# Another order of the steps in both mixers of a two-layer hybrid diffusion backbone

## The chip, the cores and the metric

The kernel runs on one core of one Trainium2 chip. The metric is the device time of one execution in microseconds (us), as the median of several runs. The weights lie in HBM and come in by DMA. Five engines work side by side, each through its own instructions in the order in which they stand in its queue: TensorE (PE, with its weight loads shown apart as PEld), VectorE (DVE), ScalarE (ACT), GpSimd (POOL) and SyncE (SP). They wait for each other by semaphores. An instruction that waits holds back everything behind it on its engine, whether that could run or not.

## What is computed

Two layers work on 256 latent tokens and 256 context tokens of width 1024. Each layer is a half-step feed-forward net (FFN), a mixer, and another half-step FFN; the last mixer and the last FFN work on the latent tokens alone. Cut to the mixer, which is all that the change touches:

```python
def mixer(hx, hc, p, cos, sin, with_ctx):
    qx, kx, vx, ux, gx, bgx, cgx, sx = jnp.split(hx @ p['w_in'], cuts, axis=-1)
    qc, kc, vc, uc, gc, bgc, cgc, sc = jnp.split(hc @ p['w_in'], cuts, axis=-1)
    # group A: attention, 8 query heads, 2 key heads, width 64; q and k RMS-normalised
    qx = apply_rope(head_rms(qx, p['q_g']), cos, sin)
    kx = apply_rope(head_rms(kx, p['k_g']), cos, sin)
    kc = head_rms(kc, p['k_g'])
    attn_x = blocked_attention(qx, concat([kc, kx]), concat([vc, vx]))
    # group B: a linear recurrence in both directions after a width-4 convolution
    hc_f = lru_dir(uc, p, 0, h0, False);  hx_f = lru_dir(ux, p, 0, hc_f[:, -1], False)
    hc_b = lru_dir(uc, p, 1, h0, True);   hx_b = lru_dir(ux, p, 1, hc_b[:, 0], True)
    lru_x = (hx_f + hx_b) * gelu(gx)
    # group C: a gated width-3 convolution
    sc_x = bgx * dw_conv(cgx * sx, p['sc_conv_w'], p['sc_conv_b'], SC_PAD)
    # each group RMS-normalised, concatenated, one projection
    out_x = merge_groups([attn_x, lru_x, sc_x], p['grp_g'], p['w_out'])
    # layer 0 does the same for the context tokens (with_ctx)
```

The two sides of the tokens are called s = 0 (context, 256 keys) and s = 1 (latent, 512 keys) below.

## The kernel before

Activations lie transposed in SBUF, features on the 128 partitions, with context and latent tokens side by side as 512 columns. Every product of fp32 matrices is made of three matmuls in a reduced format (`mm3`, lines 333 to 335): each operand is split into a high part, made by ACT (line 132), and a low part, made by DVE (line 133). This holds for the weights too: a weight block of 128x1024 (512 KB) is fetched by SP into one of seven raw buffers (`dma_to`, four blocks ahead), then ACT makes `hi` and DVE makes `lo`. `get` asks for a block by its name and splits two blocks ahead (`advance`). All blocks are fetched in the order that `plan` fixes; within a mixer `mix_units` walks the table `ORDER` for it, so the blocks of `kv`, `qp`, `sc` and `op` follow the table's order.

PSUM has eight banks of 128x512 fp32, given out in turn by `bank` to whoever asks. A product, a score, a transposition and a statistic take one each, and keep it until ACT or DVE has read it.

A mixer first makes h, the normalised and modulated input (`head`), with the first four blocks of the projection. Then it walks `ORDER[l]` (line 955). Each entry is a step, named by two letters and an index:

- `cv` convolution of the recurrence's input (ACT, DVE); `ga` its gates (two matmuls of 128x512 in fp32 on PE, line 763, then tanh, tanh, tanh, exp and square on ACT); `lr` a logarithm and an exponential (ACT), `ls` the scan (DVE), `le` its end (DVE)
- `ge` gelu (ACT, DVE)
- `kv`, `qp` the key, value and query products (PE, in four held banks each); `ka`, `qa` their statistics; `kb`, `qb` norm, rotation and split of the rows (DVE, ACT); `kc`, `qc` their transposition (PE lines 659 and 697, copied out by ACT)
- `sc` the gated convolution: i % 3 = 0, 1, 2 are its three projections
- `sm` the scores of one head: matmuls (line 832), the row maximum on DVE (`nb`, line 833), the exponential with its sum on ACT (`P`, line 836). In layer 0 `sm0` to `sm7` are side s = 0 and `sm8` to `sm23` side s = 1; layer 1 has `sm0` to `sm15`, all s = 1
- `tr` four transpositions of P on PE (line 846), copied to `PT` by DVE (line 849) and ACT (line 851) by turns
- `va` P times values (line 864, summed in a held bank); `nr` the inverse sums (reciprocal on DVE, two spreads `re` on ACT line 875, eight transpositions on PE line 882, two copies `rec` on ACT)
- `ra`, `rb` norm and merge of the attention group (squares on ACT line 895, statistic on PE line 900); `ma` the statistic of the recurrence's group (`ma1`) and of the convolution's (`ma0`) (squares `acc` and `sq` on ACT lines 359 and 362, statistic on PE line 381, then Ln and Exp on ACT and three steps on DVE); `mb` their scaling and splitting
- `op` one eighth of the output projection of these two groups (12 matmuls); it needs all four `mb`.

After the table the attention group's part of the projection follows. Ln and Tanh lie in different tables of ACT; `tanh` and `ln` (lines 573 and 578) keep them apart and put a table load where the kind changes.

The table gives the order in which the steps are written. A scheduler then places each engine's instructions; where an instruction is not ready by its reckoning it lets later ones pass. So the queue of an engine follows the table, though not word for word.

Of the kernel before, what the change touches and what calls it, by code (L numbers as in the profile page):

```python
# [26 lines left out]


ORDER = (
# [5 lines left out]
    "op5 op6 op7").split(),  # L35
# [3 lines left out]
    "tr13 tr14 tr15 ls2 ls3 le1 nr1 ma1 mb2 mb3 op0 va2 va3 op1 ra1 rb1 op2 op3 op4 op5 op6 op7").split())  # L39


P_BMOD, P_NG, P_GRP, P_FIN = 0, 144, 192, 208
# [1057 lines left out]
```

## Time and profile before

| | |
|---|---|
| median of three runs | 1728.09 us (1726.1 to 1729.63) |
| the profiled execution's own time | 1726.93 us |
| its span | 1725.1 us |
| PE busy | 1645.0 us, 95% of the span |
| DVE busy | 1128.2 us, 65% |
| ACT busy | 661.1 us, 38% |
| mean granted clock of TensorE | 0.981 of full speed |

The span is what the profiler covers, and 1.8 us more lie around it. A busy PE is not a PE at its peak, since its clock changes: 0.50 in a row means the lower of its two levels (1.2 GHz), 1.00 the upper (2.4 GHz). What matters for a change that only moves work is where PE stands idle and what it waits for there. Mixer 0 lies at 425 to 605 us in the span (after its `head`), mixer 1 at 1380 to 1505 us.

### The profile page before, as it was taken

What the parts mean: (1) busy time and instruction counts of PE and PEld (TensorE: products, weight loads), DVE (VectorE), ACT (ScalarE), POOL (GpSimd) and SP (SyncE); (2) the same over time, 40 slices, a digit from 0 to 9 for tenths busy, and PEclk for the clock granted to TensorE, in tenths of its full rate; (3) what the DMA queues carried; (4) which work ended last, traced back from release to release, by engine and by line L of the source; (5) the groups of instructions that cost most, each with busy time, mean ns of one, the idle gap of its engine ahead of it and who ended that gap; (6) DMA issues with size and microseconds to landing.
All of it is one profiled execution on the core that took longest, in us unless ns stands there. A gap on an engine that the chain in (4) does not pass through costs nothing. (4 is left out here: it accounts for less than half of the span.)

```text
span 1725.1 us, 22220 instructions
## 1 busy us (share of the span) xinstructions
PE 1645.0 (95%) x8790; PEld 1394.4 (81%) x8790; DVE 1128.2 (65%) x1869; ACT 661.1 (38%) x1036; POOL 0.2 (0%) x4
## 2 busy tenths in 40 slices
PE   7999999999986999999999999999999988799997
PEld 2888888889764698888888898888888886689997
DVE  4977756675675676686676765664556768575555
ACT  5332122324855443221223252212222359454442
POOL 0000000000000000000000000000000000000000
PEclk9999999999988999999999999999999999899999
DMA  7455645452320024455455424453444332145551
GB/s 292 166 188 185 205 144 179 168 189 90 111 73 13 29 70 159 167 188 181 147 180 179 154 98 147 159 183 113 144 145 157 112 122 86 39 155 186 183 183 39
DMA packets 67937, 246.26 MB, mean 143 GB/s; under 512 B 7668, under 2 KB 8180, under 8 KB 67576
## 3 DMA queue, kind: packets, MB, share of 16 engines
q1 hardware_dynamic: 66816, 243.82, 40.9%
q8 instruction: 69, 1.13, 0.3%
q10 hardware_dynamic: 1016, 1.01, 0.2%
q14 instruction: 36, 0.29, 0.1%
HBM read 243.76 MB, written 1.05 MB: 142 GB/s over the span
## 5 line engine op out<-in xcount | busy, mean ns | idle before, releaser
L132 ACT ACTIVATE hi<-raw 128x1024 fp32r<-128x1024 f32 x310 | 327.2, 1060 | 790.2 <-PE ps L334 593.0
L334 PE MATMUL ps<-hl,hi 128*128 128x512 f32 (+1 forms) x1664 | 584.1, 352 | 0.9 <-DVE hl L418 0.7
L333 PE MATMUL ps<-hh,hi 128*128 128x512 f32 (+1 forms) x1664 | 576.0, 352 | 9.3 <-ACT hh L417 9.1
L335 PE MATMUL ps<-hh,lo 128*128 128x512 f32 (+1 forms) x1664 | 580.9, 350 | 0.0
L133 DVE TENSOR_TENSOR lo<-raw,hi 128x1024 fp32r<-128x1024 f32 x310 | 378.7, 1224 | 195.8 <-ACT hi L132 194.0
L333 PEld LDWEIGHTS ps<-hh,hi 128*128 128x128 f32 x1664 | 313.2, 191 | 53.5 <-ACT hh L417 12.6
L334 PEld LDWEIGHTS ps<-hl,hi 128*128 128x128 f32 x1664 | 317.9, 191 | 43.5 <-DVE hl L418 3.0
L335 PEld LDWEIGHTS ps<-hh,lo 128*128 128x128 f32 x1664 | 317.9, 191 | 40.3
L258 DVE SCALAR_TENSOR_TENSOR junk<-raw,cb 128x1024 bf16<-128x1024 f32 x272 | 321.3, 1221 | 15.3 <-DMA raw<-in_wpk_dram 15.3
L333 PE MATMUL ps<-gh,hi 128*128 128x512 f32 (+1 forms) x770 | 267.7, 348 | 0.0
L334 PE MATMUL ps<-gl,hi 128*128 128x512 f32 (+1 forms) x770 | 267.2, 347 | 0.0
L335 PE MATMUL ps<-gh,lo 128*128 128x512 f32 (+1 forms) x770 | 267.1, 347 | 0.0
L496 DVE TENSOR_TENSOR gf<-gf,ps 128x512 f32<-128x512 f32 (+1 forms) x88 | 54.6, 621 | 182.2 <-PE ps L335 181.0
L333 PEld LDWEIGHTS ps<-gh,hi 128*128 128x128 f32 x770 | 145.9, 190 | 18.1
L334 PEld LDWEIGHTS ps<-gl,hi 128*128 128x128 f32 x770 | 145.9, 189 | 18.1
L335 PEld LDWEIGHTS ps<-gh,lo 128*128 128x128 f32 x770 | 145.9, 190 | 18.0
L426 DVE SCALAR_TENSOR_TENSOR xT<-ps,modT,xT 128x256 f32<-128x256 f32 x160 | 72.5, 480 | 69.0 <-PE ps L335 68.0
L417 ACT ACTIVATE hh<-ht,modT 128x256 fp32r<-128x256 f32 x88 | 41.9, 504 | 70.7 <-DVE ht L416 70.1
L362 ACT ACTIVATE sq<-xT 128x256 f32<-128x256 f32 (+1 forms) x62 | 29.0, 486 | 74.9 <-DVE xT L426 73.5
L133 DVE TENSOR_TENSOR gl<-gf,gh 128x512 fp32r<-128x512 f32 (+1 forms) x88 | 54.5, 620 | 0.7 <-ACT gh L132 0.7
L418 DVE SCALAR_TENSOR_TENSOR hl<-ht,modT,hh 128x256 fp32r<-128x256 f32 x88 | 40.6, 483 | 20.8 <-ACT hh L417 20.6
L333 PE MATMUL ps<-mh,hi 128*128 128x256 f32 (+1 forms) x160 | 50.3, 314 | 3.4 <-ACT mh L132 3.4
(181 smaller groups left out, 1228.3 us busy)
## 6 DMA issues: line engine op xcount, KB each, us to landing
raw<-in_wpk_dram SPq DMA_DIRECT2D x456, 512.0 KB, 3.3
xT<-in_xin_dram SPq DMA_DIRECT2D x2, 1024.0 KB, 9.7
lw<-in_lruw_dram SPq DMA_DIRECT2D x2, 512.0 KB
cb<-in_cc_dram SPq DMA_DIRECT2D x2, 512.0 KB, 3.6
out_dram<-y SPq DMA_DIRECT2D x2, 256.0 KB, 2.6
out_dram<-y ACTq DMA_DIRECT2D x2, 256.0 KB, 2.6
pps<-in_pp_dram ACTq DMA_DIRECT2D x1, 138.0 KB, 4.0
qkb<-in_qkg_dram ACTq DMA_DIRECT2D x1, 128.0 KB
```

What stands on the lines that cost most here:

```text
L132: act(hi, src, AF.Copy)
L133: tt(lo, src, f(hi), OP.subtract)
L258: stt(junk, raw, 1.0, CB[v], op0=OP.mult, op1=OP.mult, accum_out=mod_col(l, m, t, v))
L333: nc.tensor.matmul(ps, wh, xh, start=first, stop=False)
L334: nc.tensor.matmul(ps, wh, xl, start=False, stop=False)
L335: nc.tensor.matmul(ps, wl, xh, start=False, stop=last)
L362: act(sq[:, a:b], src, AF.Square)
L417: act(hh[:, a:b], t[:, a:b], AF.Identity, bias=mod_col(l, 3 * n, k, v))
L418: MADE.append(stt(hl[:, a:b], t[:, a:b], mod_col(l, 3 * n, k, v), f(hh[:, a:b]), op0=OP.add, op1=OP.subtract).ins)
L426: stt(xT[:, k, a:b], ps[:, a:b], mod_col(l, m, k, v), xT[:, k, a:b], op0=OP.mult, op1=OP.add)
L496: tt(gf[:, a:b], gf[:, a:b], pu[:, a:b], OP.mult)
```

## The change

Only the table `ORDER` changes. Both versions hold the same steps, 125 in layer 0 and 97 in layer 1, each once; the functions behind them, the number of instructions apart from table loads, and the bytes moved are the same. The fetch order of the weight blocks follows through `mix_units`: in layer 0 the second `kv` block now comes after two `qp` blocks, and in layer 1 the blocks of `sc0`, `kv1` and `sc1` come before those of `qp1` to `qp3`. ACT's table loads number 16 before and 18 now; both additional ones are in mixer 1.

```diff
 ORDER = (
-    ("cv0 cv1 kv0 kv1 ga0 ga1 ga3 ga2 qp0 qp1 ka0 kb0 kb1 ge0 ge1 qp2 qp3 qa0 qb0 qb1 lr0 lr1 lr2 lr3 sc0 sc1 "
...
+    ("cv0 cv1 kv0 ga1 ga0 ga2 ge0 ga3 qp0 qp1 kv1 lr0 ls0 ka0 kb1 ge1 kb0 qp2 qp3 qa0 qb0 qb1 kc0 kc3 sc0 sc1 "
...
-    ("cv0 kv0 kv1 ka0 kb0 kb1 qp0 qp1 qp2 qp3 qa1 qb2 qb3 ga0 qc4 qc5 qc6 qc7 sc0 cv1 sc1 ge0 sc2 kc0 kc1 kc2 "
...
+    ("cv0 cv1 kv0 ga0 ge0 qp0 ga3 sc0 kv1 ka0 lr3 kb1 sc1 kb0 qp1 qp2 qp3 qa1 qb2 kc2 kc3 kc1 kc0 qb3 qc4 qc5 "
...
```

The rows below are the queues of the built programs, with equal neighbours merged. First ACT in mixer 0, from the second half of the query rows (`qr`) to the first transposed P (`PT`); before:

```order
L132 ACTIVATE hi<-raw 128x1024
L132 ACTIVATE qr<-qo 128x4x64 x4
L836 ACTIVATE P,sums<-ps,nb 128x256 x2
L718 ACTIVATE cg<-ps 128x512
L836 ACTIVATE P,sums<-ps,nb 128x256 x4
L851 ACTIVATE PT<-ps 128x512
```

and now:

```order
L132 ACTIVATE qr<-qo 128x4x64 x2
L718 ACTIVATE cg<-ps 128x512
L836 ACTIVATE P,sums<-ps,nb 128x256 x4
L700 ACTIVATE qT<-ps 128x512
L836 ACTIVATE P,sums<-ps,nb 128x256 x4
L132 ACTIVATE hi<-raw 128x1024
L132 ACTIVATE qr<-qo 128x4x64 x2
L728 ACTIVATE sc<-pd,pps 128x512
L836 ACTIVATE P,sums<-ps,nb 128x256 x6
L132 ACTIVATE hi<-raw 128x1024
L851 ACTIVATE PT<-ps 128x512
```

Before, all four remaining splits of query rows stood ahead of the first exponential; now two do, and fourteen exponentials, of seven heads, stand ahead of the first `PT`.

Next PE in mixer 0, from the first statistic of a group (`acc`, `sq` times `ones`); before:

```order
L381 MATMUL ps<-acc,ones_114 128x512
L381 MATMUL ps<-sq,ones_114 128x512
L832 MATMUL ps<-kT,qT 128x512 x8
L864 MATMUL ps<-PT,vt 64x512 x4
L882 MATMUL ps<-idf,re 128x128 x8
L846 MATMUL ps<-idf,P 128x128 x16
L832 MATMUL ps<-kT,qT 128x512 x4
L900 MATMUL ps<-sq,ones_112 128x256 x4
L832 MATMUL ps<-kT,qT 128x512 x4
L846 MATMUL ps<-idf,P 128x128 x16
L381 MATMUL ps<-acc,ones_114 128x512
L381 MATMUL ps<-sq,ones_114 128x512
```

and now:

```order
L381 MATMUL ps<-acc,ones_114 128x512
L381 MATMUL ps<-sq,ones_114 128x512
L832 MATMUL ps<-kT,qT 128x512 x4
L846 MATMUL ps<-idf,P 128x128 x4
L832 MATMUL ps<-kT,qT 128x512 x4
L846 MATMUL ps<-idf,P 128x128 x12
L882 MATMUL ps<-idf,re 128x128 x8
L381 MATMUL ps<-acc,ones_114 128x512
L381 MATMUL ps<-sq,ones_114 128x512
L832 MATMUL ps<-kT,qT 128x512 x6
L864 MATMUL ps<-PT,vt 64x512 x4
L832 MATMUL ps<-kT,qT 128x512 x6
```

The second statistic has moved forward, next to the inverse sums; the attention group's own statistic (line 900) has moved out of this stretch, to behind `op3`.

Last PE in mixer 1, from the end of the query products (`lo`, `hi` times h) on; before:

```order
L335 MATMUL ps<-hi,hl 128x512
L763 MATMUL ps<-uc,lw 128x512 x2
L697 MATMUL ps<-idr,qr 128x128 x4
L333 MATMUL ps<-hh,hi 128x256
L334 MATMUL ps<-hl,hi 128x256
L335 MATMUL ps<-hh,lo 128x256
```

and now:

```order
L335 MATMUL ps<-hi,hl 128x512
L659 MATMUL ps<-idr,kr 128x128 x16
L697 MATMUL ps<-idr,qr 128x128 x2
L333 MATMUL ps<-hh,hi 128x256
L334 MATMUL ps<-hl,hi 128x256
L335 MATMUL ps<-hh,lo 128x256
```

The sixteen transpositions of keys stand where one gate step stood. The first transposition of query rows still follows directly, ahead of the next projection (`sc3` now, `sc0` before).

## Rows read from the trace of the kernel before

**Rows 1.** The page, its head and its first part: busy time of PE.

```profile
span 1725.1 us, 22220 instructions
PE 1645.0 (95%) x8790; PEld 1394.4 (81%) x8790; DVE 1128.2 (65%) x1869; ACT 661.1 (38%) x1036; POOL 0.2 (0%) x4
```

**Rows 2.** Windows: stretch, length, busy us by engine, granted clock, DMA share, GB/s.

```profile
425.00:605.00 180.00, 151.93 (x754) 116.57 (x753) 116.39 (x212) 108.29 (x221) 0.00 (x0) 0.93 0.17 59
1380.00:1505.00 125.00, 103.71 (x632) 85.34 (x631) 86.52 (x156) 80.53 (x158) 0.00 (x0) 0.90 0.22 76
```

**Rows 3.** PE's waits, 425 to 605 us: us in total, times, longest.

```profile
PE ps L846 <- ACT P L836: 10.2, 4, 8.4
PE ps L882 <- ACT re L875: 7.8, 2, 6.4
PE ps L381 <- ACT acc L359: 7.5, 2, 5.6
```

**Rows 4.** PE's waits, 1380 to 1505 us.

```profile
PE ps L381 <- ACT acc L359: 6.3, 2, 5.1
PE ps L697 <- DVE qr L133: 5.1, 1, 5.1
PE ps L846 <- ACT P L836: 4.6, 2, 2.4
PE ps L333 <- ACT mh L132: 3.4, 1, 3.4
PE ps L882 <- ACT re L875: 1.8, 1, 1.8
```

**Rows 5.** Windows: 256-wide matmuls back to back; then where the granted clock fell.

```profile
1380.00:1385.00 5.00, 5.00 (x44) 5.00 (x43) 0.00 (x0) 0.12 (x1) 0.00 (x0) 1.00 0.00 0
...
1410.00:1415.00 5.00, 0.00 (x0) 0.00 (x0) 4.93 (x14) 1.15 (x4) 0.00 (x0) 0.91 0.39 147
1415.00:1420.00 5.00, 4.93 (x29) 4.94 (x29) 3.07 (x7) 2.56 (x4) 0.00 (x0) 0.50 0.00 1
1420.00:1425.00 5.00, 5.00 (x40) 5.00 (x40) 2.56 (x3) 4.48 (x8) 0.00 (x0) 0.91 0.02 3
495.00:510.00 15.00, 9.25 (x35) 7.29 (x36) 7.01 (x16) 5.01 (x19) 0.00 (x0) 0.66 0.10 36
535.00:545.00 10.00, 5.45 (x28) 5.08 (x28) 3.21 (x5) 7.36 (x16) 0.00 (x0) 0.66 0.00 0
555.00:565.00 10.00, 6.91 (x14) 3.87 (x16) 4.05 (x9) 4.87 (x11) 0.00 (x0) 0.66 0.00 0
1465.00:1475.00 10.00, 5.31 (x20) 4.62 (x20) 7.13 (x16) 3.52 (x10) 0.00 (x0) 0.69 0.00 1
1475.00:1490.00 15.00, 8.59 (x29) 4.96 (x30) 5.82 (x14) 6.50 (x15) 0.00 (x0) 0.64 0.00 1
```

**Rows 6.** Timelines of PE and ACT, 1407 to 1416 us: start, us, instruction.

```profile
1408.07 1.88 PE L763 MATMUL ps<-uc,lw 128*128 128x512 f32 x4
1415.07 0.81 PE L697 MATMUL ps<-idr,qr 128*128 128x128 f32 x4 [5.12 <-DVE qr L133]
...
1414.02 0.72 ACT L132 ACTIVATE qr<-qo 128x256 fp32r<-128x256 f32 x2 [3.12 <-DVE qo L630]
```

**Rows 7.** Timeline of ACT, 438 to 448 us: gates of mixer 0.

```profile
438.81 1.28 ACT L576 ACT_TABLE_LOAD   x1
...
443.48 1.25 ACT L576 ACTIVATE th<-ps,hb 128x512 f32<-128x512 f32 x2
...
446.85 1.25 ACT L576 ACTIVATE th<-ps,hb 128x512 f32<-128x512 f32 x2
```

**Rows 8.** Groups by line, whole span: row maximum, exponential and its sum.

```profile
L833 DVE TENSOR_REDUCE nb<-ps 128x1 f32<-128x512 f32 (+1 forms) x40 | 26.1, 685 | 15.1 <-PE ps L832 15.0
L836 ACT ACTIVATE P<-ps,nb 128x512 f32<-128x512 f32 (+1 forms) x48 | 29.0, 614 | 8.8 <-DVE nb L833 8.8
L836 ACT ACTIVATION_READ_ACCUMULATOR P<-ps,nb 128x1 f32 x48 | 9.8, 205 | 0.0
```

More of the change, by code (lines that the diff above doesn't have):

```diff
@@ L29 @@
 ORDER = (
[5 rows of a table removed]
-    "op5 op6 op7").split(),
[3 rows of a table removed]
-    "tr13 tr14 tr15 ls2 ls3 le1 nr1 ma1 mb2 mb3 op0 va2 va3 op1 ra1 rb1 op2 op3 op4 op5 op6 op7").split())
[5 rows of a table added]
+    "va4 ra1 rb1").split(),
[3 rows of a table added]
+    "va2 ls0 le0 lr2 ls2 le1 ma1 tr3 va3 mb2 va1 mb3 op0 op1 op2 ra1 rb1 op3 op4 op5 op6 op7").split())
 P_BMOD, P_NG, P_GRP, P_FIN = 0, 144, 192, 208
```

12 rows, old and new, of the table ORDER are left out of this document.

## The prediction

> **What bounds the kernel now.** PE does: it is busy for 1645.0 of 1725.1 us [rows 1]. Since the change only moves steps of the two mixers, I read the windows of these two stretches next. In mixer 0 (425 to 605 us) PE is busy for 151.9 of 180 us, in mixer 1 (1380 to 1505 us) for 103.7 of 125 us [rows 2]: 28.1 and 21.3 us of idle time, which is the better part of the 80 us that PE idles at all. DVE and ACT are far from full there (116 and 108 us, 87 and 81 us [rows 2]), so none of the three is a floor: the time goes where one of them stands in front of something that is not ready. PE's waits name the places. In mixer 0 they are a P that comes late (8.4 us at the longest), the spread sums `re` (6.4) and the squares of a group (5.6) [rows 3]; in mixer 1 the squares (5.1), the first query rows (5.1) and a merge (3.4) [rows 4]. Nearly all end on ACT.
>
> **The clock adds to it.** Around six of these waits the granted clock falls to 0.50, the lower level. In the clearest, PE is idle from 1409.95 to 1415.07 us [rows 6]; the clock gives 0.91, 0.50 and 0.91 in the three windows of 5 us [rows 5], that is 6.8 us at the lower level, from 1414.1 to 1420.9, of which 5.8 us after work has begun again. All six places together have 47.6 us at the lower level (twice the length times what is missing to 1.00, summed over the windows [rows 5]). About 5.5 us in each, 33 us in all, are spent working; at half speed that costs 16.5 us, 7.9 in mixer 0 and 8.5 in mixer 1. So 36.0 us in mixer 0 and 29.8 in mixer 1 are lost to order: 65.8 us, the most that a permutation can give.
>
> **What the change costs in itself.** Matmuls, copies and bytes are the same. The weight blocks come in another order, but each is still asked for four ahead, the DMA engines are busy for 0.17 and 0.22 of these stretches [rows 2], and PE waits for no DMA in them [rows 3, 4]: nothing. ACT gets two more table loads in mixer 1, 1.28 us each [rows 7]; 2.6 us, priced with wait (i) below.
>
> The Trainium skill speaks against this edit: ScalarE: Activation LUTs, section Rules for kernel authors, wants all work of one table set done before a switch, and budgets about 2.7 us for each. The trace has 1.28 [rows 7] and decides; by the page's figure the two loads would be 5.4 us, and the gain below smaller by up to 2.8 us.
>
> **What PE will meet instead.** I followed the three queues of the changed program through both mixers with the spacings of the rows: 0.114 us for a 256-wide matmul (44 in 5 us [rows 5]), twice that for 512, one gate on ACT 3.37 us (446.85 - 443.48 [rows 7]), a row maximum 0.69 and an exponential 0.61 with 0.20 for its sum [rows 8]. Where a producer's sum is later than PE's, the difference is a wait. None of them stands in the old trace; the bounds follow the list.
>
> Mixer 0:
> (a) All four gates now stand ahead of the query products, whose four banks come free only with the tanh of the third and fourth gate. ACT needs a load, three gates, a square and a tanh, 1.3 + 10.1 + 0.5 + 0.6 = 12.5 us; PE has three gate steps (1.88 each [rows 6]), 23 narrow and six wide matmuls, 5.6 + 2.6 + 1.4 = 9.6 us. Queued behind are all of `qp` and the rest of `kv1`. About 3.2 us, new.
> (b) `qc2` behind `sc0` and `sc1`: these 48 matmuls and eight transpositions cover 11.8 us, the query rows need about 12.8. 1.0 us.
> (c) The wait of 8.4 us goes: between the scores and the first `tr` now stand 48 projection matmuls (10.9 us), and the exponentials are no longer behind all query rows on ACT.
> (d) The recurrence's statistic still waits for its squares: 1.4 us (before: 7.5 - 5.6 = 1.9 [rows 3]). `tr8` stands close behind `sm9`, whose maximum and exponential (1.3 us) queue behind two others on ACT: 1.6 us. Inverse sums 0.5, second statistic 1.2, `op0` behind the last merge 1.0, the attention statistics 0.5.
> (e) From `op2` on projections lie between everything. Together 10.4 us. My sums go by spacing; a chain loses more at each hop, by an estimate of mine some 0.1 us, five or six hops a wait: 3 us. **13.4 us stay of 36.0.**
>
> Mixer 1:
> (f) The first query transposition still follows the products directly. From the end of the products (1408.07) to the first rows (1415.07) it takes 7.0 us [rows 6]; the cover was one gate step of 1.88, and is now sixteen transpositions, some 1.4. So this wait stays, at 5.5 us, and the clock falls again: 2.9 us.
> (g) Seven scores and a projection fill all eight banks; `sc2` waits for the copy of `sc4`, which ACT makes behind two exponentials: 1.6 us.
> (h) Behind it PE has filler (`sc2`, `sc5`), and the waits for P (4.6 us [rows 4]) go.
> (i) ACT then has two gates (6.7 us), two loads (2.6) and nine exponentials (some 0.66 each) to do, and PE comes to `tr0` and `tr1` ahead of a free bank and of the P of `sm4`: 4.3 us.
> (j) First statistic 1.5, `tr12` 0.5, inverse sums 0.5, second statistic 0.2, `op0` 0.8 (the merge's 3.4 us before [rows 4], since `va` and `tr3` now lie behind the statistic). Together 17.8 us, and 2 us for hops. **19.8 us stay of 29.8.**
>
> Sum: 22.6 + 10.0 = 32.6 us. From the profiled execution's own 1726.9 us this gives 1694.3; the median of the runs shown is 1.2 us above it, so 1696 us (rounded).
>
> Bounds: the short waits, (a) to (e) and (g) to (j), may be covered altogether (the cover in each is within 3 us of the chain), or twice as long (a chain of 6 hops behind a few more entries of ACT's queue). I take the middle because PE is behind its producers at some of them and ahead at others. Nothing here can be a gain beyond 65.8, and (f) does not go.
>
> **Rivals.** *The waits move.* ACT is the engine on which nearly all waits end [rows 3, 4], and its work is unchanged. If the short waits come out twice as long, 13.4 and 11.4 us more are lost and 7.8 us are gained: 1720. For it: PE is now early at many places, each by one or two us. Against: ACT is busy for only 108 of 180 us in mixer 0.
> *All but two go.* Only (f), (a) and (i) stay, 16 us: 49 us gained, 1679. For it: projections between nearly all steps of mixer 0. Against: eight banks.
> *The order does not matter*: PE waits elsewhere for the same sum, 1728. Against: the 8.4 and 5.6 us had nothing in front of them that now has 10.9 us.
> *Slower: the clock stays low.* Between 1475 and 1490 us PE was busy for 8.6 of 15 us, its waits were 1.8, 1.2 and 3.4 us, and the clock was 0.64 [rows 4, 5]. Short waits in a row can thus do what one long one does. If the 25 us from the first statistic to `op0` in mixer 0 and the 25 us before `op0` in mixer 1 run at the lower level, some 20 us of work in each take 40: 40 us lost against 32.6 gained, 1735. [...] Against: the wait of 2.4 us in mixer 1 [rows 4] stands by itself between full stretches, and no fall of the clock goes with it (rows 5 has all six), and PE is busy for four fifths in my sums.
>
> **Chances.** The sum as worked out, a gain of 20 to 44 us: 0.66. Waits move: 0.15. All but two go: 0.08. No change: 0.05. Slower: 0.06. The likeliest gives 1696 us. The range takes the first case (1684 to 1708), most of the second gain and half of the moved waits: 1680 to 1715. A measurement of this kernel tells about 0.2% (3.5 us) from no change; faster by more 0.89, within 0.05, slower by more 0.06.
>
> **What would show it.** In the new profile PE's wait for P ahead of the first `PT` (8.4 us) is gone; the window of mixer 0 shows some 23 us less from its first key product to its end, and at most one dip of the clock; a new wait of line 333 for a tanh stands some 15 us behind the first key products; in mixer 1 line 697 still waits for `qr` by 5 to 6 us with a dip of the clock behind it, and line 846 waits for P or a bank by some 4 us. I am wrong if mixer 0 has waits of over 4 us, if the clock falls there more than once, or if line 697 in mixer 1 no longer waits.

## The result and the profile after

The changed kernel takes 1687.18 us (median of four runs, 1685.05 to 1687.82) against 1727.89 us for the kernel before: a ratio of 0.9766, with a 95% interval of 0.9753 to 0.9778. That is 40.7 us, or 2.3%, less. Measured a second time, it was 0.9779 (0.9764 to 0.9793). The forecast was 1696 us, with a range of 1680 to 1715.

The head of the page of after answers to [rows 1]:

```profile
span 1685.2 us, 22230 instructions
PE 1636.9 (97%) x8790; PEld 1388.3 (82%) x8790; DVE 1126.6 (67%) x1869; ACT 663.4 (39%) x1038; POOL 0.2 (0%) x4
```

PE, DVE and ACT do the same work in a span that is 39.9 us shorter; what went is PE's idle time and its time at the lower clock. To say where, one needs marks that both traces have. PE's statistic over 256 columns at the end of a stage is one. It stands last ahead of mixer 0 and first behind it, and last ahead of mixer 1 and first behind it. The timeline of PE in the kernel before (start, length, instruction):

```profile
401.58 0.60 PE L381 MATMUL ps<-acc,ones 128*128 128x256 f32 x2
...
620.69 0.60 PE L381 MATMUL ps<-acc,ones 128*128 128x256 f32 x2
...
1361.62 0.59 PE L381 MATMUL ps<-acc,ones 128*128 128x256 f32 x2
...
1517.36 0.70 PE L381 MATMUL ps<-acc,ones 128*128 128x256 f32 x2 [0.53 <-DVE acc L366]
```

and in the changed kernel:

```profile
402.49 0.60 PE L381 MATMUL ps<-acc,ones 128*128 128x256 f32 x2
...
591.48 0.60 PE L381 MATMUL ps<-acc,ones 128*128 128x256 f32 x2
...
1332.41 0.59 PE L381 MATMUL ps<-acc,ones 128*128 128x256 f32 x2
...
1477.33 0.70 PE L381 MATMUL ps<-acc,ones 128*128 128x256 f32 x2 [0.53 <-DVE acc L366]
```

From the first mark to the second it was 219.1 us and is 189.0: **mixer 0 gained 30.1 us**. From the second to the third it is 740.9 us in both. From the third to the fourth it was 155.7 and is 144.9: **mixer 1 gained 10.8 us**. Below, the time from the first mark to the end of the span is called the net time: 1323.5 us before (1725.1 - 401.58), 1282.7 after.

The windows of the two mixers in after, as in [rows 2] (mixer 0 up to its first 256-wide products, mixer 1 up to the place that 1505 us was before), and then the windows in which the granted clock fell, as in [rows 5]:

```profile
425.00:576.00 151.00, 145.96 (x764) 114.09 (x763) 114.24 (x204) 107.11 (x215) 0.00 (x0) 0.99 0.22 74
1350.80:1465.00 114.20, 101.61 (x632) 83.32 (x631) 84.98 (x153) 82.73 (x160) 0.00 (x0) 0.93 0.26 88
520.00:525.00 5.00, 3.25 (x14) 2.85 (x14) 3.17 (x5) 3.78 (x9) 0.00 (x0) 0.66 0.00 0
1390.00:1405.00 15.00, 9.56 (x54) 8.09 (x53) 10.16 (x22) 7.15 (x17) 0.00 (x0) 0.77 0.22 70
1425.00:1440.00 15.00, 9.42 (x31) 5.17 (x30) 11.13 (x20) 12.91 (x27) 0.00 (x0) 0.66 0.05 19
```

PE idles for 5.0 us in mixer 0 (28.1 before) and 12.6 in mixer 1 (21.3 before). At the lower level of the clock it spends 3.4 us in mixer 0 (23.8 before) and some 17 in mixer 1 (23.8 before). So 23.1 of mixer 0's 30.1 us are idle time, and PE's busy time between the two marks shrinks by the other 7.0 (191.0 to 184.0 us), for the same matmuls at a higher clock; in mixer 1 it is 8.7 and 2.1.

PE's waits in after, first in mixer 0, then in mixer 1 (line and what it waited for: us in total, times, longest), against [rows 3, 4]:

```profile
PE ps L381 <- ACT acc L359: 2.9, 2, 1.7
PE ps L846 <- ACT P L836: 2.1, 1, 2.1
```

```profile
PE ps L697 <- DVE qr L133: 5.2, 1, 5.2
PE ps L846 <- ACT PT L851: 2.5, 1, 2.5
PE ps L846 <- ACT P L836: 2.4, 2, 1.9
PE ps L381 <- ACT acc L359: 1.2, 1, 1.2
...
PE ps L333 <- ACT mh L132: 0.3, 1, 0.3
...
```

The waits of 8.4, 6.4 and 5.6 us are gone from mixer 0. In mixer 1 the wait for the first query rows stands as it stood, and behind it one for a bank and a P; what went is most of the 6.3 us for the squares, of the 3.4 for a merge, and the 1.8 for `re`. No run below takes the new order of layer 1 apart to say which moves did that: what gained the 10.8 us of mixer 1 is read from the waits alone.

### The profile page after: what moved, and what is told of

The parts are those of the page before. It is cut to its first block, busy times and chain, and to the rows that moved or that the text cites. A ratio compares the mean times of both kernels' runs of the same rounds, so it can differ in the third digit from the quotient of the medians.

```text
span 1685.2 us, 22230 instructions
## 1 busy us (share of the span) xinstructions
PE 1636.9 (97%) x8790; PEld 1388.3 (82%) x8790; DVE 1126.6 (67%) x1869; ACT 663.4 (39%) x1038; POOL 0.2 (0%) x4
## 4 chain that ended last, share of the span: by engine, by line
PE 90%; DVE 5%; ACT 3%; DMA 1%; issue 1%; ACTq 0%; DVEq 0%; SPq 0%
PE ps L333 28%; PE ps L334 28%; PE ps L335 28%; DVE lo L133 1%; PE ps L864 1%; DVE junk L258 1%; PE ps L381 1%; PE ps L832 1%; PE ps L846 1%; PE ps L763 1%; ACT hh L417 1%; DMA xT<-in_xin_dram 1%; DVE hl L418 1%; DVE ht L416 1%; ACT hi L132 1%
## 5 line engine op out<-in xcount | busy, mean ns | idle before, releaser
L333 PEld LDWEIGHTS ps<-hh,hi 128*128 128x128 f32 x1664 | 312.7, 190 | 53.1 <-ACT hh L417 12.6
L258 DVE SCALAR_TENSOR_TENSOR junk<-raw,cb 128x1024 bf16<-128x1024 f32 x272 | 321.2, 1219 | 13.7 <-DMA raw<-in_wpk_dram 13.6
L132 ACT ACTIVATE gh<-gf 128x512 fp32r<-128x512 f32 (+1 forms) x88 | 50.5, 574 | 3.6 <-DVE gf L496 3.6
```

The lines of the kernel that those rows point to most:

```text
L132: act(hi, src, AF.Copy)
L258: stt(junk, raw, 1.0, CB[v], op0=OP.mult, op1=OP.mult, accum_out=mod_col(l, m, t, v))
L333: nc.tensor.matmul(ps, wh, xh, start=first, stop=False)
```

## The experiments

The program's start, up to the first of these marks, which no edit touches, takes 401 to 407 us from run to run (the last section has the rows). The net time of the changed kernel, though, was 1282.7 and 1282.8 us in its two profiled runs. Between the marks, mixer 0 in the new order takes 188.4 to 189.1 us in six traces, and mixer 1 in the old order 155.3 to 155.7 in seven. So the table gives, besides the timed ratio to before, the net time of each profiled run, which tells differences of over 1 us apart where the ratio can't. It is that of one execution each.

| run | ratio to before, 95% interval | net time, us | against |
|---|---|---|---|
| before | 1 | 1323.5 | |
| after, twice | 0.9766 (0.9753 to 0.9778), 0.9779 (0.9764 to 0.9793) | 1282.7, 1282.8 | before: -40.8 |
| l0_only | 0.9818 (0.9796 to 0.9840) | 1292.4 | before: -31.2 |
| cover_tr0 | 0.9955 (0.9938 to 0.9972) | 1316.9 | before: -6.6 |
| rows_late | 0.9944 (0.9925 to 0.9962) | 1312.9 | before: -10.6 |
| merges_late | 0.9963 (0.9943 to 0.9982) | 1316.5 | before: -7.1 |
| ma0_fwd | 1.0000 (0.9984 to 1.0016) | 1323.9 | before: +0.4 |
| rows_merges_ma0 | 0.9915 (0.9899 to 0.9932) | 1310.3 | before: -13.2 |
| fill_before | 0.9974 (0.9953 to 0.9994) | 1322.9 | before: -0.7 |
| merges_early | 0.9820 (0.9805 to 0.9836) | 1293.2 | after: +10.4 |
| cover_qc4 | 0.9750 (0.9732 to 0.9769) | 1282.5 | after: -0.2 |
| q_first | 0.9782 (0.9766 to 0.9799) | 1285.7 | after: +3.0 |
| ga1_d | 0.9770 (0.9755 to 0.9784) | 1285.5 | after: +2.7 |

All but one are moves of steps in the table `ORDER`, written in its words.

### One layer alone

The new first line of `ORDER` with the old second one.

> The new order in layer 0 alone, layer 1 as before. The prediction's sum: 22.6 us less than before, about 1705 us. Read from the trace of the changed kernel, where the statistic behind mixer 0 (first matmul of line 381 with 256 columns) comes 29.2 us earlier although the first key products came 0.9 us later: 30.1 us less, about 1698. Rival: the two mixers depend on each other through the fetch order of the blocks and the clock, so that one alone brings next to nothing (1720 and more) or nearly all (1690).

It took 1697.78 us. By the marks mixer 0 gains 30.7 us here (30.1 in the changed kernel) and mixer 1 next to nothing (155.3 us, 155.7 before), so what the order of layer 0 brings does not hang on that of layer 1. The new order of layer 1 was not run alone; 9.6 us of net time are what is left for it.

> The changed kernel once more, beside the next two for comparison on one chip. 0.9766 of before, 1686 to 1690 us.

It took 1690.11 us.

### The wait of 8.4 us: two ways to remove it

More cover for it on PE:

```diff
-  ... sm0 sc3 sm2 sm1 tr0 tr1 sc4 sm3 sm4 ...
+  ... sm0 sc3 sm2 sm1 sc4 tr0 tr1 sm3 sm4 ...
```

> The kernel before, with the one step sc4 moved ahead of the first tr in layer 0: 24 matmuls (5.6 us) more lie between the scores and the first transposition of P. Theory (the cover decides): the wait of 8.4 us falls to 2.8 and the fall of the clock behind it goes or halves, 5.6 to 8.3 us less, 1720 to 1722. Rival (the wait moves): sc4 is missing behind the first tr, the same time is lost at the next tr or at the inverse sums, 1727 to 1729.

Or its producers earlier in the queues of ACT and DVE:

```diff
-  ... qa1 qb2 qb3 sm0 sc3 sm2 sm1 tr0 tr1 ...
+  ... qa1 sm0 sc3 sm2 sm1 qb2 qb3 tr0 tr1 ...
```

> The kernel before, with qb2 and qb3 moved behind sm1 in layer 0: four splits of query rows, and their rotations on DVE, stand behind the first exponentials instead of ahead; PE's queue stays as it was but for one matmul. Theory (ACT's and DVE's order decides): P of the third score is ready some 2 us behind its matmuls, the wait of 8.4 us falls to 2 or 3, and the clock stays up: 6 to 9 us less, 1719 to 1722. Rival (the rows are then late in their turn): line 697 or the scores behind it wait for qr by as much, 1727 to 1729.

PE's waits from 425 us on, first of cover_tr0 (to 610 us), then of rows_late (to 605 us):

```profile
...
PE ps L846 <- ACT P L836: 4.9, 4, 2.9
...
```

```profile
PE ps L882 <- ACT re L875: 7.8, 2, 6.4
PE ps L381 <- ACT acc L359: 7.7, 2, 5.6
...
PE ps L846 <- ACT P L836: 2.4, 3, 1.0
```

and the window of rows_late in which the clock was 0.66 before [rows 5]:

```profile
495.00:510.00 15.00, 14.25 (x78) 11.73 (x77) 14.54 (x26) 8.71 (x25) 0.00 (x0) 1.00 0.21 69
```

Both go as the theories had it, rows_late by more than its 6 to 9 us. Twenty-four matmuls of cover take the longest wait for P from 8.4 to 2.9 us; the other order of ACT and DVE takes it to 1.0. The longest waits further on, 6.4 and 5.6 us, stay as they were in both. So the wait did not move, and 10.6 us are its price: 7.8 us of waits for P (10.2 before [rows 3], 2.4 here), and the rest with the fall of the clock, which is gone.

### The waits of 6.4 and 5.6 us: merges ahead of exponentials

Moving only the second statistic forward:

```diff
-  ... va1 nr0 tr8 tr9 ... tr14 tr15 ma0 mb0 mb1 sm20 ...
+  ... va1 nr0 ma0 tr8 tr9 ... tr14 tr15 mb0 mb1 sm20 ...
```

> The kernel before, with the one step ma0 moved forward to behind nr0 in layer 0 (its squares pass ACT ahead of two PT, two exponentials and the attention group's squares). Theory (the wait of 5.6 us is ACT's queue ahead of the squares, not late data): the wait falls to 1 or 2 us, the clock stays up there, and mixer 0 is 5 to 7 us shorter: 1721 to 1724. Rival (PE only meets the next late producer, the exponentials behind the statistic): within 2 us of before, the same time spent at lines 846 and 900.

The theory fell. PE's wait at line 900 in before, and then its waits from 425 to 610 us in ma0_fwd:

```profile
PE ps L900 <- ACT sq L895: 2.4, 1, 2.4
```

```profile
...
PE ps L900 <- ACT sq L895: 4.5, 1, 4.5
PE ps L381 <- ACT acc L359: 3.1, 2, 1.9
PE ps L832 <- ACT P L836: 2.5, 1, 2.5
```

The wait of 5.6 us at line 381 is down to 1.2 as expected, but the time is back as 2 us more at line 900 and a new 2.5 at line 832, and PE still spends some 7 us at the lower level there. The queue of ACT in before shows what holds up one of these producers, the spreads `re`. Its timeline there, from the merge behind the first statistic to the spreads:

```profile
...
535.01 1.29 ACT L132 ACTIVATE mh<-uc 128x512 fp32r<-128x512 f32 x2 [4.22 <-DVE uc L924]
...
538.86 1.15 ACT L875 ACTIVATE re<-ri 128x512 f32<-128x512 f32 x2
```

ACT stands idle for 4.2 us ahead of the split of a merge, which waits for DVE; four exponentials and the spreads `re`, for which PE waits 6.4 us, are queued behind it. The table of before writes each merge (`mb2 mb3`, `rb0`, `mb0 mb1`) directly behind its statistic. Moving the merges alone leaves PE's queue in the built program as it is, word for word:

```diff
-  ... ma1 mb2 mb3 sm12 sm13 sm10 sm11 ... ra0 rb0 sm16 sm17 ... ma0 mb0 mb1 sm20 sm21 sm18 sm19 ...
+  ... ma1 sm12 sm13 sm10 sm11 mb2 mb3 ... ra0 sm16 sm17 rb0 ... ma0 sm20 sm21 sm18 sm19 mb0 mb1 ...
```

> The kernel before, with the merges moved away from their statistics in layer 0: mb2 and mb3 behind sm11, rb0 behind sm17, mb0 and mb1 behind sm19. PE's queue is the same word for word; on ACT four, two and four exponentials now stand ahead of the splits mh instead of behind. In the trace of before these splits wait 4.2, 2.5 and 4.9 us for DVE, with the exponentials and the spreads re queued behind them. Theory (a merge right behind its statistic holds up ACT): the exponentials fill these idle times, the wait of 6.4 us for re falls to 2 or 3, that for the squares of the convolution's group falls too, and the time from the last statistic ahead of mixer 0 to the end of the kernel, 1323.5 us in the trace of before, is 6 to 10 us shorter; about 1719 to 1723. Rival (the exponentials wait for scores and maxima anyway, PE being late itself): within 2 us of before.

The same stretch of ACT in merges_late, and PE at the spreads:

```profile
530.91 0.67 ACT L836 ACTIVATE P<-ps,nb 128x512 f32<-128x512 f32 x1
...
535.22 1.29 ACT L132 ACTIVATE mh<-uc 128x512 fp32r<-128x512 f32 x2 [0.61 <-DVE uc L924]
536.42 1.13 ACT L875 ACTIVATE re<-ri 128x512 f32<-128x512 f32 x2
```

```profile
537.09 2.06 PE L882 MATMUL ps<-idf,re 128*128 128x128 f32 x8 [3.76 <-ACT re L875]
```

The exponentials fill the gap, the spreads come 2.4 us earlier, and the wait falls from 6.4 to 3.8 us (2 or 3 were expected): 7.1 us of net time for moves on ACT and DVE alone. The reverse, in the changed kernel:

```diff
-  ... ma1 sm13 sm14 ... nr0 ma0 sm22 sm17 mb2 mb3 sm21 mb0 va0 sm15 mb1 ...
+  ... ma1 mb2 mb3 sm13 sm14 ... nr0 ma0 mb0 mb1 sm22 sm17 sm21 va0 sm15 ...
```

> The changed kernel with the merges moved back next to their statistics in layer 0: mb2 and mb3 directly behind ma1, mb0 and mb1 directly behind ma0. Theory: ACT idles some 4 us ahead of each pair of splits, the exponentials behind them come later, and PE waits that much longer at the inverse sums and behind the second statistic: 4 to 9 us slower than the changed kernel in its last run (1282.8 us from the last statistic ahead of mixer 0 to the end of the kernel). Rival (the new order has projections as cover there): within 2 us of it.

It loses 10.4 us, more than the 4 to 9 expected. ACT's waits and PE's in merges_early, 425 to 605 us:

```profile
ACT mh L132 <- DVE sc L924: 5.4, 1, 5.4
...
ACT mh L132 <- DVE uc L924: 4.2, 1, 4.2
...
```

```profile
PE ps L846 <- ACT P L836: 6.1, 1, 6.1
...
```

The idle times of 4.2 and 5.4 us are ACT's again, and PE waits 6.1 us for a P queued behind the split that waited 4.2. With that the clock falls for longer: 13.6 us at the lower level in mixer 0, 3.4 in after.

Last, the three moves on before together (`qb2 qb3`, the merges, `ma0`):

> The kernel before with three kinds of moves in layer 0: the query rows qb2 and qb3 behind sm1, the three groups of merges away from their statistics, and ma0 forward to behind nr0. Theory (these are what the new order gains in mixer 0): the query rows alone took 10.6 us off, ma0 alone none; with the merges out of ACT's way the three together take off 17 to 25 us of the 30 that the new order of layer 0 takes off; 1704 to 1712. Rival (cover by projections between the steps of attention, which these moves don't add, is what gains): no more than 13 us, 1716.

It took 13.2 us off, less than the 17.3 of its parts added up, and less than half of the 31 that the new order of layer 0 brings. PE still waits 4.5 us at line 900 and 3.8 at line 882 in it, waits that after doesn't have, and 13.6 us of mixer 0 run at the lower level. So the rival has the size right: the larger part, some 18 us, lies in moves that these three don't make. The new order has four parts of the output projection (`op0` to `op3`, 48 matmuls) among the scores and transpositions and ahead of the attention group's own statistic (`ra0`), where before has none. That this cover is what gains the rest was argued only, and not measured.

### What the clock alone is worth

```diff
...
+            for _ in range(FILL.get((l,) + key, 0)):
+                nc.tensor.matmul(ps, idr, h.at(0, (0, 512))[0] if key[0] == "qc" else kT[0], start=True, stop=True)
...
```

> The kernel before, with matmuls of no use (identity times a row that is there, 128x512, results overwritten) put in front of five of the six waits behind which the granted clock fell: 33 ahead of the first tr, 24 ahead of the inverse sums, 20 ahead of the second statistic in layer 0; 18 ahead of the first query transposition and 18 ahead of the first statistic in layer 1. Each lot is some 1 us shorter than the wait. Theory (the clock costs 16.5 us in itself): the granted clock stays at 1.00 there, the waits end at the same time, and the work behind them runs at full speed: five sixths of 16.5, 13.7 us less, 1714. Rival (the half clock is hidden, since PE would wait for ACT and DVE there anyway): the clock stays up and the time stays at 1728. If the clock falls all the same, nothing is told.

Windows of fill_before; the program's start took 5 us longer here, so each place is some 2 to 5 us later than in [rows 5]:

```profile
495.00:510.00 15.00, 14.30 (x70) 11.47 (x70) 11.95 (x29) 6.66 (x21) 0.00 (x0) 1.00 0.11 36
...
565.00:585.00 20.00, 16.25 (x77) 12.54 (x74) 9.38 (x16) 10.52 (x24) 0.00 (x0) 0.83 0.00 1
...
1410.00:1420.00 10.00, 9.12 (x48) 6.88 (x47) 9.38 (x23) 3.47 (x9) 0.00 (x0) 1.00 0.32 105
1445.00:1455.00 10.00, 7.76 (x38) 7.54 (x39) 5.26 (x9) 6.84 (x15) 0.00 (x0) 0.66 0.16 55
...
```

and one of PE's waits in mixer 1, at the line that is 882 in the other kernels (1.8 us in [rows 4]):

```profile
PE ps L894 <- ACT re L885: 3.6, 1, 3.6
```

The filler kept the clock at 1.00 at the filled places of mixer 0 and at the first query rows, but the clock then fell at places that had no fall before (0.83 from 565 to 585 us, 0.66 from 1445 to 1455). So the lower level did not go: in mixer 0 it shrank from 23.8 to 10.3 us, in mixer 1 it was 23.9 as before. By the marks the run gains 3.1 us in mixer 0 (216.0 instead of 219.1), where the prediction's price for the 13.5 us that went would be some 4.5 of its 7.9, and loses 2.5 in mixer 1 (158.2 instead of 155.7), where by the condition that was set ahead nothing is told. Timed, it is 1 to 8 us, not 13.7. The trace is of an execution of 1731.44 us with a mean clock of 0.982; the ten lie between 1719.43 and 1731.44 us, the shortest at 0.990, and where the clock fell in the others is not on record. What the lower level costs by itself thus stays open. That PE gets ahead at full clock and waits the longer at the next producer is one reading of the 3.6 us, and not shown.

### The wait that stayed: first query rows in mixer 1

More cover ahead of it; the query products ahead of `kv1`; or a gate step earlier, where ACT has a gap (all on the changed kernel):

```diff
-  ... kc1 kc0 qb3 qc4 qc5 sc3 qc7 qc6 ...
+  ... kc1 kc0 qb3 sc3 qc4 qc5 qc7 qc6 ...
```

> The changed kernel, with the step sc3 (24 matmuls, 2.9 us at full clock) moved ahead of qc4 in layer 1, so that it lies between the key transpositions and the first query transposition. Theory (the wait of 5.2 us is want of cover): PE waits 2.3 to 3.5 us there (a weight split of DVE's, 1.2 us, now stands ahead of the rows), the second half of the rows is there when PE asks, and all behind it is 2 to 4 us earlier: 2 to 4 us less than the changed kernel in the same session. Rival (ACT sets the pace from there to the statistic, 25 us with hardly a pause): PE waits as much less here as it waits more for P and PT, and the time stays within 1 us.

```diff
-  ... sc0 kv1 ka0 lr3 kb1 sc1 kb0 qp1 qp2 qp3 qa1 qb2 kc2 kc3 kc1 kc0 qb3 qc4 qc5 sc3 qc7 qc6 ga1 ...
+  ... sc0 qp1 qp2 qp3 qa1 kv1 qb2 ka0 lr3 qb3 kb1 sc1 kb0 qc4 qc5 sc3 qc7 qc6 ga1 kc2 kc3 kc1 kc0 ...
```

> The changed kernel, with qp1 to qp3 and their statistic ahead of kv1 in layer 1, and the key transpositions behind sc3 and ga1. Theory (the wait belongs to the seven us from products to rows, of whichever products come last): the query rows are ready when PE has done kv1 and sc1 (8.4 us), so the wait of 5.2 us goes with the fall of the clock (8 to 9 us together); the key rows then have sc3, ga1 and the query transpositions (6.2 us) for cover and come up to 4 us late: 3 to 8 us less than the changed kernel. Rival (DVE, busy for 14.5 of the 15 us from 1380, carries both rows and can't be reordered): the wait moves to line 659 at its full length, within 1 us of the changed kernel.

```diff
-  ... qp3 qa1 qb2 ... sc3 qc7 qc6 ga1 sm13 ...
+  ... qp3 qa1 ga1 qb2 ... sc3 qc7 qc6 sm13 ...
```

> The changed kernel with the gate step ga1 moved forward in layer 1, from behind the query transpositions to behind the query statistic, where ACT has 3.1 us with nothing to do. It needs a table load, three tanh, an exponential and a square, 4.7 us. Theory (ACT sets the pace from the first exponential to the statistic of the convolution's group): the first rows come 1.6 us later, but the exponentials start 3 to 4 us earlier, and the waits of 2.5 us for PT and 1.9 us for P behind them shrink: 1 to 4 us less than the changed kernel (1282.8 us from the last statistic ahead of mixer 0 to the end). Rival (the first query rows set the pace): 1 to 2 us more.

PE's waits in mixer 1 in cover_qc4, in q_first, and in ga1_d:

```profile
PE ps L697 <- DVE qr L133: 4.0, 2, 2.8
PE ps L846 <- ACT PT L851: 2.5, 1, 2.5
PE ps L846 <- ACT P L836: 2.4, 2, 1.9
...
```

```profile
PE ps L832 <- ACT kT L662: 3.9, 1, 3.9
PE ps L659 <- ACT kr L132: 3.9, 1, 3.9
...
```

```profile
PE ps L697 <- DVE qr L133: 9.3, 1, 9.3
...
```

In cover_qc4 the first wait is down to 2.8 us as the theory has it, but the net time is the same: 2.5 and 1.9 us behind it, for PT and P, stand unchanged, and ACT is busy for 12.91 of the 15 us from 1425 us in after. Its median, 1684.22 us, is below that of the changed kernel in the same session, 1690.11. The net times of the two profiled runs (1282.5 and 1282.8, of 1688.09 and 1690.60 us in all) show none of this; the other runs, down to 1682.42 us, have no trace, so that it stays open whether this order is faster. In q_first the 5.2 us become 3.9 at line 659 and 3.9 at line 832: the keys are then the rows that come late. In ga1_d PE waits 9.3 us for the first rows, 4.1 more, and the waits for PT and P behind shrink by 0.5 and 0.2. By the net times, of one execution each, none of the three theories held. Only in cover_qc4 is it the rival as it was written (within 1 us); q_first and ga1_d lost 3.0 and 2.7 us, more than their rivals said. That the rows' chain of DVE and ACT sets the time here fits all three, but was not shown by itself, and no traced execution was shorter by more than 0.2 us.

## Why the prediction was right, by its steps

The sign, the place and the mechanism were right: the time is PE's idle time behind ACT, and it went where the sum said. The sum said 32.6 us and it was 40.7. Mixer 1 was nearly met (10.0 and 10.8); 7.5 of the 8 us are in mixer 0 (22.6 and 30.1).

**What goes (c).** The wait of 8.4 us, by the cover and by the order of ACT and DVE: each was measured by itself, on the old order, and leaves 2.9 and 1.0 us of it.

**What stays in mixer 0.** Of 13.4 us that I let stand, 5.0 are idle time, and one fall of the clock of 3.4 us. Three terms of (d) were met: 1.4 was 1.7, the 1.6 for `tr8` was 2.1, the second statistic's 1.2 was 1.2. The steps that failed are (a), (b), the 1.0 us for `op0`, the 0.5 us each for the inverse sums and the attention statistics, and the 3 us for hops: none of them came. PE ran from 425 to 510 us without a wait:

```profile
425.00:510.00 85.00, 85.00 (x461) 70.77 (x460) 70.31 (x127) 69.53 (x137) 0.00 (x0) 1.00 0.31 101
```

In (a) I let all of `qp` wait until the third and the fourth gate had both been read. But the four banks are not asked for at once. The timeline of ACT at the third and the fourth gate in after, and of PE at the first product of `qp` and at the first into its third bank:

```profile
441.82 1.25 ACT L576 ACTIVATE th<-ps,hb 128x512 f32<-128x512 f32 x2
...
445.71 1.25 ACT L576 ACTIVATE th<-ps,hb 128x512 f32<-128x512 f32 x2
```

```profile
442.54 0.50 PE L333 MATMUL ps<-hi,hh 128*128 128x512 f32 x1
...
446.55 0.40 PE L333 MATMUL ps<-hi,hh 128*128 128x512 f32 x1
```

The first product of `qp` starts at 442.54 us, when ACT has read the first bank of the third gate. In the built queue 17 matmuls then go into the first two banks, which take 4.0 us, and only the next needs the first bank of the fourth gate, which ACT reads from 445.71 us. PE's own 9.6 us in (a) were met: from its first gate step at 432.85 us to 442.54 it is 9.7. A chain is to be held against the first bank that is needed, not against the last. (The terms of (a) as written give 12.5 - 9.6 = 2.9 us, not 3.2.) The 2 and 3 us for hops were an allowance without a row; it should have been left out.

**What stays in mixer 1.** (f) was forecast as 5.5 us and a fall of the clock like the one before, 6.8 us at the lower level, priced at 2.9: it is 5.2, and again 6.8 us at the lower level (of the 15 us from 1390). (i) was forecast as 4.3 and is 2.5 for a bank and 1.9 for P. The bank in (g) was no wait. What I had missed is a second fall of the clock behind (i), 10.2 us at the lower level; it took about what the unneeded terms had left over. That the sum for mixer 1 was nearly met is thus in part luck: two errors of it cancel. Mixer 1 now has four table loads where it had two; one of them in ACT's timeline of after:

```profile
1405.19 1.28 ACT L576 ACT_TABLE_LOAD   x1
```

It took 1.28 us, and so did the one at 1424.54, as the loads of before; the tanh behind it starts at 1406.49, 1.30 us after the load began. The Trainium skill (ScalarE: Activation LUTs, Rules for kernel authors) budgets 2.7 us for a switch; the trace does not agree, and the change gained with two more of them.

**The clock.** The 16.5 us were added to the idle time as if each could be had by itself. In the changed kernel, with most waits gone, PE's busy time shrank by 7.0 us in mixer 0, near the 7.9, and by 2.1 in mixer 1, where two falls stay. What the clock is worth without the waits is not settled: fill_before moved the falls more than it removed them. (With three places of 5.5 us in each mixer the price is 8.3 us for each; the prediction's 7.9 and 8.5 are not derived.)

**What I had not seen** is that a merge behind its statistic holds up ACT. The prediction names no cause for the wait of 6.4 us and lets the inverse sums come down to 0.5 without one; the runs show 7.1 us for moving the merges away, and 10.4 for moving them back.

**The rivals.** *All but two go* (49 us) was as far from the 40.8 us as the sum: in mixer 0 it was the better account, but for (a), and in mixer 1 the worse. Waits that move as a whole, and an order that doesn't matter, are out by the trace of after; the single move of `ma0` shows that the first can well happen. A clock that stays low did not come: the short waits from 511 to 526 us pulled it down for one window of 0.66.

## What to carry to other kernels

Follow an in-order queue for its own head that waits: a wait on PE named after ACT was a gap on ACT in front of work that could have run, and moving the merges behind the ready exponentials was worth 7.1 us, where moving a statistic that PE waited for, and not the merge in front of it, was worth nothing. Test a move both ways, alone on the old order and taken back in the new one, since gains of moves do not add up (13.2 us of 17.3 here). Cover put in front of a wait need not help: 6.6 us came of it in cover_tr0, and nothing in the traced run of cover_qc4, where the waits behind stayed as they were.

## What the runs showed of the hardware that was not expected

The granted clock can be held up with matmuls of no use during a wait: 1.00 instead of 0.66 over 15 us (fill_before), though it then fell elsewhere. And the first 50 us of the program run at a clock that differs from run to run, in code that is the same everywhere. The window of the first 50 us in before, and in fill_before:

```profile
0.00:50.00 50.00, 38.23 (x104) 17.23 (x105) 28.23 (x69) 24.51 (x44) 0.20 (x4) 0.93 0.73 273
```

```profile
0.00:50.00 50.00, 38.07 (x81) 15.34 (x82) 24.10 (x59) 23.79 (x42) 0.20 (x4) 0.83 0.67 252
```

With a clock of 0.93 there the first mark is reached at 401.6 us, with 0.83 at 406.5; in the two runs of the changed kernel it was 402.5 us with 0.93 and 405.9 with 0.86. The DMA rate is lower as well (252 GB/s instead of 273), and which of the two comes first was not tried. From 50 us to 395 us the clock is 1.00 in all fourteen traces, so that the difference arises in these first 50 us. Five us are as much as a single move gains; marks inside the trace take them out.
